# A hybrid decoder trunk on one core: small constants moved to the sync queue, the first memory and weight pieces halved, 8 leading products instead of 18

## The chip, the core and the metric

The kernel runs on one core of one Trainium2 chip. A core has five engines that run their own instruction streams in order and meet through semaphores: TensorE (matrix products; PE in the profile, its weight loads PEld), VectorE (DVE), ScalarE (ACT), GpSimd (POOL) and SyncE (SP, which here only issues transfers). Sixteen transfer engines carry data between the chip's main memory and the on-chip memory. Transfers can be issued from the sync engine, from ScalarE and from GpSimd.

The metric is the device time of one execution in microseconds (us). Before the change the median of three runs is 1012.1 us (1011.76 to 1013.38).

## What is computed

A decoder trunk of two layers on 256 tokens with 1024 channels, in float32, and a memory of 256 rows. Cut to its frame:

```python
mem_kv = rms_norm(mem, mem_norm_g) @ mem_w_kv
for i in range(2):
    x = x + 0.5 * swiglu(rms_norm(x, ffn1_norm_g[i]), ffn1_w_in[i], ffn1_w_out[i])
    hn = rms_norm(x, mix_norm_g[i])
    # layer 0: mLSTM heads; layer 1: sliding-window attention with learned sinks
    # both: 4 heads that attend to the memory, through mem_k and mem_v
    x = x + jnp.concatenate([y_tok, y_mem], axis=-1) @ w_out
    x = x + 0.5 * swiglu(rms_norm(x, ffn2_norm_g[i]), ffn2_w_in[i], ffn2_w_out[i])
```

`swiglu` multiplies by a gate half and an up half of `w_in` (2 x 2816 columns), forms silu(gate) * up, and multiplies by `w_out`. Nearly all the time is in these products and in the projections.

## The kernel before

**Products in three parts.** Every float32 weight and activation is split into a rounded high half and the remainder, the low half. A product is then three passes of TensorE: high by high, high by low, low by high (`mm3`, lines 224 to 227). A weight piece is 128 partitions by 4 chunks by 256 columns, 512 KB. `wtile` (line 216) fetches it through the sync queue into one of 5 raw buffers (`wr`), and `split` (line 206) makes the halves: ScalarE casts the high half (`wh`, line 211), VectorE subtracts to get the low half (`wl`, line 212). There are 8 buffers of each half, so the splits can run some pieces ahead of TensorE. A raw buffer is free for the next fetch when VectorE has made the low half.

**Who sets the order.** TensorE and the sync engine run in the order in which the program emits their instructions (`manual_schedule`, line 987). For ScalarE, VectorE and GpSimd a scheduler at build time fixes the order from its own model of times; on the chip these engines then run that order strictly. `issue_after` lets a block of instructions be placed no earlier than a given one. `Weave` interleaves the main chain of products with side chains (`spawn`) by an estimate of TensorE's time.

**The start.** `memory()` (line 400) computes keys and values of the memory. It first issues 18 leading products on a cleared tile (`WARM`, line 58; line 406), whose result is not used. Then it fetches the memory in four blocks of two chunks (`memT`, line 410, 256 KB each); `split_gain` (line 239) scales a chunk by the norm's gain and splits it, the high half on ScalarE (line 132), the low half on VectorE (line 241). The weights `mem_w_kv` are used in four groups of 256 columns, each 8 chunks deep. Group 0's first four chunks are fetched as two pieces of two chunks behind memory block 0, its last four as one piece behind block 2. Its first half is multiplied by `first_part` (line 323, products at line 334), which takes all high-by-high products of a piece first, so that the low halves may come later; the second half and the other groups go through `part` with `mm3`. Behind the fetches of group 1 stand those of `con` (identity, frequencies, masks), then of the other groups and the activations `xT`. The statistics of the memory's norm are a small product (line 231) and a chain on VectorE and GpSimd (lines 250, 251).

**The small constants.** `late_constants` (line 182) fetches the attention mask (196 KB), the gate bias, the sinks, the positions and two norm gains of 16 values through GpSimd's queue, copies the mask and the identity to bf16 (`maskb`, `identb`), and makes `gcut`, `nsink` and `gqk` on VectorE. It is spawned by the first feed-forward after its group 5, but the scheduler places work that waits for nothing earlier: in the profile GpSimd issues five of the fetches within the first 5 us, and the mask's at 51 us.

**The feed-forward.** `ffn_in` (line 471) runs 11 groups; a group takes four weight pieces, called quarters here (two halves of depth, each for gate and up), 24 products each, into two banks of PSUM. When a group's products are done, `hidden` (line 473), the gating, runs: two products with the norm's row on VectorE (line 476), SiLU on ScalarE, two products with the up half on VectorE (line 479), then `split_plain`: a cast on ScalarE (line 245) and a subtraction on VectorE (line 246).

```python
            for ps in waiting:
                hidden(ps)
            waiting.clear()
            if mid is not None and gi == 5:
                wv.spawn(mid())
```

Of the kernel before, what the change touches and what calls it, by code (L numbers as in the profile page):

```python
# [19 lines left out]
P = 128  # L20
# [34 lines left out]
           keys=5.5, keys_d=7.2, query=9.0, head=1.5, head_m=2.5, head_p=9.3, head_o=4.0)  # L55


WARM = 18


class Weave:
# [37 lines left out]
def tile_trunk(ctx: ExitStack, tc: tile.TileContext, a, out):  # L99
# [80 lines left out]
    gqk = mk(cst, [P, 2], F32, "gqk")  # L180

    def late_constants():
        nc.gpsimd.dma_start(mask.rearrange("p a b -> p (a b)")[:, :3 * P], a["mask"])
        nc.gpsimd.dma_start(gbias, a["a_gate_b"][0].rearrange("(s h) -> h s", h=4))
        nc.gpsimd.dma_start(sink, a["b_sinks"][0].partition_broadcast(P))
        nc.gpsimd.dma_start(posi, a["positions"][0].rearrange("(h p) -> p h", p=P))
        nc.vector.tensor_copy(identb, ident)
        nc.vector.tensor_copy(maskb, mask.rearrange("p a b -> p (a b)")[:, :3 * P])
        for i, (n, r) in enumerate((("b_q_norm_g", G_BQ), ("b_k_norm_g", G_BK))):
            nc.gpsimd.dma_start(gblk[:, i], a[n][0, :ROT].partition_broadcast(P))  # L190
            nc.vector.tensor_copy(gcut[:, i:i + 1], g(r))
        for e in range(2):
            nc.vector.memset(gcut[e * 64:e * 64 + ROT], 1.0)
        nc.vector.tensor_scalar(nsink, sink, -1.0, None, op0=ALU.mult)
        tt(out=gqk, in0=gcol[:, G_XQ:G_XQ + 2], in1=gcol[:, G_XK:G_XK + 2], op=ALU.mult)
        return
        yield

    def g(i):
        return gcol[:, i:i + 1]  # L200
# [20 lines left out]
    def wcols(w, c0, kh):  # L221
        return wtile(w.rearrange("(k p) f -> p k f", p=P)[:, kh * 4:(kh + 1) * 4, c0:c0 + 256], 4)
# [93 lines left out]
    class Group:  # L316
# [3 lines left out]
            self.ps, self.rows, self.xh, self.xl = halves(mo()), rows, xh, xl  # L320
            self.w, self.c0 = w, c0

        def first_part(self, wt):

            n = 4 // len(wt)
            for i, m, k in ((i, m, k) for q in range(len(wt)) for i in range(3) for m in range(2)
                            for k in range(q * n, q * n + n)):
                w = [t[:, k % (4 // len(wt)), m * P:(m + 1) * P] for t in wt[k * len(wt) // 4]]
                x = (self.xh, self.xl)[i == 1][k // 2][:, k % 2]
                s, mv = (w[i == 2], x) if not self.rows else (None, None)  # L330
                if self.rows:
                    ms = slice(m * P, (m + 1) * P)
                    s, mv = x[:, ms], wt[k * len(wt) // 4][i == 2][:, k % (4 // len(wt))]
                nc.tensor.matmul(self.ps[:, m], s, mv, start=i == 0 and m == 0 and k == 0, stop=False,
                                 skip_group_check=True)
                wv.now += 0.109
            yield

        def part(self, kh, wt=None):
            wt = wt or wcols(self.w, self.c0, kh)  # L340
            wt = wt if isinstance(wt, list) else [wt]
            for m in range(2):
                ms = slice(m * P, (m + 1) * P)
                for k in range(4):
                    kc = kh * 4 + k
                    h, l = self.xh[kc // 2][:, kc % 2], self.xl[kc // 2][:, kc % 2]
                    wh, wl = (w[:, k % (4 // len(wt))] for w in wt[k * len(wt) // 4])
                    if self.rows:
                        mm3(self.ps[:, m], h[:, ms], l[:, ms], wh, wl,
                            start=kc == 0 and m == 0, stop=kc == 7)  # L350
                    else:
                        mm3(self.ps[:, m], wh[:, ms], wl[:, ms], h, l,
                            start=kc == 0 and m == 0, stop=kc == 7)
                yield

# [44 lines left out]
    def memory():  # L400

        idle = tmp().rearrange("p a b -> p (a b)")[:, :T].bitcast(BF16)
        nc.vector.memset(idle, 0.0)
        bank = mo()
        for i in range(WARM):
            nc.tensor.matmul(bank, idle[:, :P], idle, start=True, stop=True, skip_group_check=True)
        wkv = a["mem_w_kv"]
        mh, ml, wfirst = [], [], []
        for c2 in range(4):
            nc.sync.dma_start(memT[c2], a["memT"][:, 2 * c2:2 * c2 + 2])  # L410
            hi, lo = unit(F32R), unit(F32R)
            for m in range(2):
                split_gain(memT[c2][:, m], g(G_MEM + 2 * c2 + m), hi[:, m], lo[:, m])
            mh.append(hi)
            ml.append(lo)
            if c2 == 0:
                v = wkv.rearrange("(k p) f -> p k f", p=P)
                wfirst.append([wtile(v[:, k:k + 2, 0:256], 2) for k in (0, 2)])
            if c2 == 2:
                wfirst.append(wcols(wkv, 0, 1))  # L420
        norm = Norm(G_MEM, rows=False)

        def keys(gi, kr):
            nc.scalar.copy(kT[gi], turn(kr))
            return
            yield

        for gi in range(2):
            gr = Group(wkv, gi * 256, mh, ml, rows=True)
            for kh in range(2):  # L430
                if gi == 0 and kh == 0:
                    yield from gr.first_part(wfirst[0])
                else:
                    yield from gr.part(kh, wfirst[kh] if gi == 0 else None)
            if gi == 0:
                first = gr
                continue
            nc.sync.dma_start(con, a["con"])
            with tc.issue_after(last[0].ins):
                for c2 in range(4):  # L440
                    norm.square(memT[c2], c2 == 0)
            norm.fold()
            wv.spawn(norm.chain(), LAT['mnorm'])
            gv = Group(wkv, 512, mh, ml, rows=True)
            yield from gv.all()
            for c2 in range(4):
                nc.sync.dma_start(xT[c2], a["xT"][:, 2 * c2:2 * c2 + 2])
            yield norm.ready
            hsc = head_scales(norm.rc, P, False)
            for i, q in enumerate((first, gr)):  # L450
                kr = tmp()
                head_norm(kr, q.ps, 2, hsc)
                wv.spawn(keys(i, kr), LAT['mkeys'] + 1.5 * i)
        for gi in range(2):
            if gi == 0:
                gr = gv
            else:
                gr = Group(wkv, 768, mh, ml, rows=True)
                yield from gr.all()
            for h in range(2):  # L460
                act(vM[:, h, gi * 256:(gi + 1) * 256], gr.ps[:, h], AF.Copy, scale=norm.rc[:, h:h + 1])
            if gi == 0:
                with tc.issue_after(last[0].ins):
                    for c2 in range(4):
                        x0.put(xT[c2])
                wv.spawn(x0.chain(LAT['x0_b']), LAT['x0'])
# [560 lines left out]
```

## Time and profile before

| | |
|---|---|
| median of 3 runs | 1012.1 us (1011.76 to 1013.38) |
| the profiled execution: its time, its span | 1012.23 us, 1010.4 us |
| VectorE's low halves, 128x1024 (line 212), each | 1196 ns mean over all forms |
| ScalarE's high halves (line 211), each | 1031 ns mean over all forms |
| weight fetches of 512 KB for the memory's keys, issue to landing | 8.0 us median |
| transfers over the span | 182.70 MB, mean 181 GB/s |

A row of the timeline reads: start and duration in us, engine, line of the kernel, operation, tile written <- tiles read, shapes, count; in brackets the engine's idle time before it and what ended that. A row of the busy times by stage reads: stretch and its length, then the busy us of each engine with the count of instructions, the granted clock, the share of the transfer engines, and GB/s. Rows of the transfer queues read: packets, MB, share of the sixteen engines' time. TensorE's products overlap in its pipeline, so a product shown as 0.28 us costs TensorE less than that: the distance between starts is its pace.

### The profile page before, as it was taken

Reading aid. Unit: us, or ns where it says so; the run is one execution under the profiler, and the core shown is the slowest. Engines: PE = TensorE matmul, PEld = TensorE weight load, DVE = VectorE, ACT = ScalarE, POOL = GpSimd, SP = SyncE. Lnnn points to the kernel's source line nnn. Section 1 sums busy time; section 2 is a strip of 40 time slices with the busy share of each in tenths; the row PEclk is TensorE's granted clock in tenths of the full one; section 3 lists DMA queues with packets and bytes.
Section 4 is the critical chain, followed back from the end, with each engine's and each line's share of the span. In section 5 each row is a group of like instructions: output and inputs, shape, how many; then the busy total and the mean of one; then the engine's idle time right before and its main releaser. Section 6 shows DMA issues by size and latency. Waiting matters only on the chain.

```text
span 1010.4 us, 20624 instructions
## 1 busy us (share of the span) xinstructions
PE 998.5 (99%) x8594; PEld 980.2 (97%) x8594; DVE 655.5 (65%) x1063; ACT 519.5 (51%) x764; POOL 35.7 (4%) x32
## 2 busy tenths in 40 slices
PE   8999999999999999999999999999999999999998
PEld 7999999999999999999999999999987899999998
DVE  6866665577856676665558666656787766666551
ACT  7754445446656554444445544544557754454440
POOL 1200000000001000000000000000121000000000
PEclk9999999999999999999999999999999999999999
DMA  9776656666644566665676666567541347666550
GB/s 308 242 245 200 192 180 185 199 183 179 184 139 133 167 210 195 200 189 170 192 206 205 189 191 201 173 197 198 182 131 66 100 131 220 198 189 185 188 170 21
DMA packets 173204, 182.70 MB, mean 181 GB/s; under 512 B 7124, under 2 KB 168328, under 8 KB 173112
## 3 DMA queue, kind: packets, MB, share of 16 engines
q1 hardware_dynamic: 171872, 179.60, 58.3%
q10 hardware_dynamic: 1016, 1.58, 0.5%
q8 instruction: 67, 1.10, 0.5%
q0 software_dynamic: 224, 0.22, 0.2%
q14 instruction: 25, 0.20, 0.1%
HBM read 180.32 MB, written 1.05 MB: 180 GB/s over the span
## 4 chain that ended last, share of the span: by engine, by line
PE 94%; DVE 3%; ACT 1%; DMA 1%; POOL 0%; issue 0%; SPq 0%; ACTq 0%
PE bank L225 30%; PE bank L226 30%; PE bank L227 30%; PE bank L231 2%; PE bank L236 1%; ACT u L132 1%; DVE wl L212 1%; DMA wr<-in_mem_w_kv_dram 1%; PE bank L961 1%; POOL col L379 0%; DVE col L930 0%; DVE u L383 0%; DVE col L591 0%; PE bank L925 0%; DVE u L946 0%
## 5 line engine op out<-in xcount | busy, mean ns | idle before, releaser
L212 DVE TENSOR_TENSOR wl<-wr,wh 128x1024 fp32r<-128x1024 f32 (+1 forms) x347 | 414.7, 1196 | 279.8 <-ACT wh L211 279.0
L211 ACT CAST wh<-wr 128x1024 fp32r<-128x1024 f32 (+1 forms) x347 | 356.8, 1031 | 393.1 <-PE bank L226 368.9
L225 PE MATMUL bank<-xh,wh 128*128 128x256 f32 x1544 | 429.1, 278 | 0.0
L226 PE MATMUL bank<-xl,wh 128*128 128x256 f32 x1544 | 426.8, 276 | 0.0
L227 PE MATMUL bank<-xh,wl 128*128 128x256 f32 x1544 | 426.8, 276 | 0.0
L226 PEld LDWEIGHTS bank<-xl,wh 128*128 128x128 f32 x1544 | 290.3, 188 | 0.1
L225 PEld LDWEIGHTS bank<-xh,wh 128*128 128x128 f32 x1544 | 290.0, 188 | 0.1
L227 PEld LDWEIGHTS bank<-xh,wl 128*128 128x128 f32 x1544 | 289.9, 188 | 0.0
L225 PE MATMUL bank<-u,wh 128*128 128x256 f32 x896 | 249.3, 278 | 0.0
L226 PE MATMUL bank<-u,wh 128*128 128x256 f32 x896 | 247.6, 276 | 0.0
L227 PE MATMUL bank<-u,wl 128*128 128x256 f32 x896 | 247.6, 276 | 0.0
L225 PEld LDWEIGHTS bank<-u,wh 128*128 128x128 f32 x896 | 168.2, 188 | 1.9 <-issue 1.7
L226 PEld LDWEIGHTS bank<-u,wh 128*128 128x128 f32 x896 | 168.4, 188 | 0.1
L227 PEld LDWEIGHTS bank<-u,wl 128*128 128x128 f32 x896 | 168.3, 188 | 0.0
L225 PE MATMUL bank<-wh,xh 128*128 128x256 f32 x208 | 59.7, 287 | 0.0
L226 PE MATMUL bank<-wl,xh 128*128 128x256 f32 x208 | 57.9, 278 | 0.0
L227 PE MATMUL bank<-wh,xl 128*128 128x256 f32 x208 | 57.9, 278 | 0.0
L476 DVE TENSOR_TENSOR t<-bank,rb 128x256 f32<-128x256 f32 x88 | 36.6, 420 | 7.3 <-PE bank L227 7.3
L225 PEld LDWEIGHTS bank<-wh,xh 128*128 128x128 f32 x208 | 39.1, 188 | 0.5 <-issue 0.3
L226 PEld LDWEIGHTS bank<-wl,xh 128*128 128x128 f32 x208 | 39.1, 188 | 0.1
L227 PEld LDWEIGHTS bank<-wh,xl 128*128 128x128 f32 x208 | 39.0, 187 | 0.0
L479 DVE TENSOR_TENSOR t<-t,bank 128x256 f32<-128x256 f32 x88 | 32.7, 412 | 1.8 <-ACT t L132 1.8
(171 smaller groups left out, 657.5 us busy)
## 6 DMA issues: line engine op xcount, KB each, us to landing
wr<-in_ffn_w_in_dram SPq DMA_DIRECT2D x176, 512.0 KB, 3.6
wr<-in_ffn_w_out_dram SPq DMA_DIRECT2D x80, 512.0 KB, 3.5
wr<-in_a_w_in_dram SPq DMA_DIRECT2D x28, 512.0 KB, 3.9
wr<-in_b_w_in_dram SPq DMA_DIRECT2D x14, 512.0 KB, 4.6
wr<-in_a_w_out_dram SPq DMA_DIRECT2D x12, 512.0 KB, 3.3
wr<-in_b_w_out_dram SPq DMA_DIRECT2D x12, 512.0 KB, 3.4
wr<-in_ffn_w_out_dram SPq DMA_DIRECT2D x16, 256.0 KB, 2.8
wr<-in_mem_w_kv_dram SPq DMA_DIRECT2D x7, 512.0 KB, 8.0
```

The source lines that it names most:

```text
L132: ins = nc.scalar.activation(*args, **kw)
L211: last[0] = nc.scalar.copy(hi[:, i * n:(i + 1) * n], src[:, i * n:(i + 1) * n])
L212: tt(out=lo[:, i * n:(i + 1) * n], in0=src[:, i * n:(i + 1) * n], in1=hi[:, i * n:(i + 1) * n].bitcast(F32), op=ALU.subtract)
L225: nc.tensor.matmul(ps, wh, xh, start=start, stop=False, skip_group_check=True)
L226: nc.tensor.matmul(ps, wh, xl, start=False, stop=False, skip_group_check=True)
L227: nc.tensor.matmul(ps, wl, xh, start=False, stop=stop, skip_group_check=True)
L231: nc.tensor.matmul(ps, lhsT, rhs, start=start, stop=stop, skip_group_check=True)
L236: nc.tensor.transpose(ps, src, ident[:k, :k])
L476: tt(out=t[:, m], in0=ps[m][:, :T], in1=x.rb, op=ALU.mult)
L479: tt(out=t[:, m], in0=t[:, m], in1=ps[m][:, T:], op=ALU.mult)
L961: nc.tensor.matmul(o[es[e], cs], vr[:, i, js], pTs[e][:, src], start=i == 0, stop=i == 1, skip_group_check=True)
```

## The change

- `late_constants` fetches its six constants through the sync queue. They stand in the sync engine's order where the routine is spawned: behind the fetch of the first quarter of group 6 of the first feed-forward. The copies and small operations on VectorE are placed after the latest weight cast at that point (`issue_after`). `gqk` is made in `memory()` instead, when `con` is fetched.
- Memory block 0 is fetched as two chunks, each followed by the weights of that chunk (128 KB each, one chunk deep). Blocks 1 to 3 stay whole, each followed by the weights of its two chunks. So group 0's weights come as five pieces of 1, 1, 2, 2 and 2 chunks, in the order of use.
- `first_part` takes a list of such pieces and is used for both halves of group 0; it now also ends the accumulation. `part` loses the case of several pieces.
- The leading products fall from 18 to 8.

```diff
-WARM = 18
+WARM = 8
...
     def late_constants():
-        nc.gpsimd.dma_start(mask.rearrange("p a b -> p (a b)")[:, :3 * P], a["mask"])
-        nc.gpsimd.dma_start(gbias, a["a_gate_b"][0].rearrange("(s h) -> h s", h=4))
-        nc.gpsimd.dma_start(sink, a["b_sinks"][0].partition_broadcast(P))
-        nc.gpsimd.dma_start(posi, a["positions"][0].rearrange("(h p) -> p h", p=P))
-        nc.vector.tensor_copy(identb, ident)
-        nc.vector.tensor_copy(maskb, mask.rearrange("p a b -> p (a b)")[:, :3 * P])
-        for i, (n, r) in enumerate((("b_q_norm_g", G_BQ), ("b_k_norm_g", G_BK))):
-            nc.gpsimd.dma_start(gblk[:, i], a[n][0, :ROT].partition_broadcast(P))
-            nc.vector.tensor_copy(gcut[:, i:i + 1], g(r))
...
+        nc.sync.dma_start(mask.rearrange("p a b -> p (a b)")[:, :3 * P], a["mask"])
+        nc.sync.dma_start(gbias, a["a_gate_b"][0].rearrange("(s h) -> h s", h=4))
+        nc.sync.dma_start(sink, a["b_sinks"][0].partition_broadcast(P))
+        nc.sync.dma_start(posi, a["positions"][0].rearrange("(h p) -> p h", p=P))
+        for i, n in enumerate(("b_q_norm_g", "b_k_norm_g")):
+            nc.sync.dma_start(gblk[:, i], a[n][0, :ROT].partition_broadcast(P))
+        with tc.issue_after(last[0].ins):
+            nc.vector.tensor_copy(identb, ident)
+            nc.vector.tensor_copy(maskb, mask.rearrange("p a b -> p (a b)")[:, :3 * P])
+            for i, r in enumerate((G_BQ, G_BK)):
+                nc.vector.tensor_copy(gcut[:, i:i + 1], g(r))
+            for e in range(2):
+                nc.vector.memset(gcut[e * 64:e * 64 + ROT], 1.0)
+            nc.vector.tensor_scalar(nsink, sink, -1.0, None, op0=ALU.mult)
...
+        def first_part(self, kh, wts):
+
+            k0 = kh * 4
+            for nk, (wh, wl) in wts:
+                for i, m, k in ((i, m, k) for i in range(3) for m in range(2) for k in range(nk)):
+                    kc = k0 + k
+                    x = (self.xh, self.xl)[i == 1][kc // 2][:, kc % 2]
+                    nc.tensor.matmul(self.ps[:, m], x[:, m * P:(m + 1) * P], (wh, wl)[i == 2][:, k],
+                                     start=i == 0 and m == 0 and kc == 0, stop=i == 2 and kc == 7,
+                                     skip_group_check=True)
+                    wv.now += 0.109
+                k0 += nk
             yield
...
+        def lead(k, nk):
+            wfirst[k // 4].append((nk, wtile(v[:, k:k + nk, 0:256], nk)))
+
         for c2 in range(4):
-            nc.sync.dma_start(memT[c2], a["memT"][:, 2 * c2:2 * c2 + 2])
             hi, lo = unit(F32R), unit(F32R)
             for m in range(2):
+                if c2 == 0:
+                    nc.sync.dma_start(memT[c2][:, m], a["memT"][:, m])
+                elif m == 0:
+                    nc.sync.dma_start(memT[c2], a["memT"][:, 2 * c2:2 * c2 + 2])
                 split_gain(memT[c2][:, m], g(G_MEM + 2 * c2 + m), hi[:, m], lo[:, m])
+                if c2 == 0:
+                    lead(m, 1)
             mh.append(hi)
             ml.append(lo)
-            if c2 == 0:
-                v = wkv.rearrange("(k p) f -> p k f", p=P)
-                wfirst.append([wtile(v[:, k:k + 2, 0:256], 2) for k in (0, 2)])
-            if c2 == 2:
-                wfirst.append(wcols(wkv, 0, 1))
+            if c2 > 0:
+                lead(2 * c2, 2)
...
             nc.sync.dma_start(con, a["con"])
+            query_key_gain()
```

## The prediction, made before the changed kernel was run

> **What bounds the kernel now.** The page comes first: the engine table, then the chain of work that ended last.
>
> ```profile
> span 1010.4 us, 20624 instructions
> PE 998.5 (99%) x8594; PEld 980.2 (97%) x8594; DVE 655.5 (65%) x1063; ACT 519.5 (51%) x764; POOL 35.7 (4%) x32
> ...
> PE 94%; DVE 3%; ACT 1%; DMA 1%; POOL 0%; issue 0%; SPq 0%; ACTq 0%
> ```
>
> TensorE sets the time. A change to loads or splits counts only where TensorE is not fed, so the busy times by stage come next.
>
> ```profile
> 1.00:5.00 4.00, 3.75 (x9) 1.34 (x10) 0.60 (x8) 1.22 (x2) 3.14 (x5) 1.00 0.62 136
> 5.00:9.00 4.00, 3.89 (x18) 2.12 (x16) 1.45 (x4) 2.74 (x6) 0.00 (x0) 1.00 1.02 233
> 9.00:15.00 6.00, 4.77 (x33) 4.00 (x32) 5.33 (x10) 4.58 (x8) 0.00 (x0) 1.00 1.08 387
> 30.00:240.00 210.00, 210.00 (x1847) 209.87 (x1847) 139.74 (x184) 107.98 (x133) 4.94 (x4) 1.00 0.68 204
> ```
>
> After the times come busy us and counts of PE, PEld, DVE, ACT and POOL, then clock, DMA share and GB/s. From 30 to 240 us, which holds the whole first feed-forward, TensorE is never idle. The idle time in reach is at the start, so the timeline of the first 20 us is third.
>
> ```profile
> 1.25 6.36 PE L406 MATMUL bank<-t 128*128 128x512 bf16 x18 [1.25 <-DVE t L403]
> ...
> 5.41 0.91 ACT L132 ACTIVATE u<-u,gcol 128x256 fp32r<-128x256 f32 x2 [3.18 <-DMA u<-in_memT_dram]
> 5.50 0.15 PEld L406 LDWEIGHTS <-t 128*128 128x128 bf16 x1 [0.28 <-issue]
> 5.92 1.19 PEld L406 LDWEIGHTS <-t 128*128 128x128 bf16 x6 [0.28 <-issue]
> 6.22 1.12 ACT L211 CAST wh<-wr 128x512 fp32r<-128x512 f32 x2
> 7.26 1.94 PE L334 MATMUL bank<-wh,u 128*128 128x256 f32 x8
> 7.55 0.17 DVE L194 TENSOR_SCALAR nsink<-sink 128x16 f32<-128x16 f32 x1 [4.46 <-DMA sink<-in_b_sinks_dram]
> ...
> 10.90 1.05 ACT L211 CAST wh<-wr 128x1024 fp32r<-128x1024 f32 x1 [0.99 <-DMA wr<-in_mem_w_kv_dram]
> 11.98 1.23 DVE L212 TENSOR_TENSOR wl<-wr,wh 128x1024 fp32r<-128x1024 f32 x1 [0.67 <-ACT wh L211]
> ...
> 12.88 1.05 ACT L211 CAST wh<-wr 128x1024 fp32r<-128x1024 f32 x1
> 13.26 0.39 PE L226 MATMUL bank<-wl,u 128*128 128x256 f32 x1 [0.87 <-DVE wl L212]
> 13.96 1.23 DVE L212 TENSOR_TENSOR wl<-wr,wh 128x1024 fp32r<-128x1024 f32 x1
> 14.24 1.05 ACT L211 CAST wh<-wr 128x1024 fp32r<-128x1024 f32 x1 [0.30 <-DMA wr<-in_mem_w_kv_dram]
> 15.32 1.22 DVE L212 TENSOR_TENSOR wl<-wr,wh 128x1024 fp32r<-128x1024 f32 x1
> 16.43 0.28 PE L225 MATMUL bank<-wh,u 128*128 128x256 f32 x1
> ...
> 17.84 0.28 PE L225 MATMUL bank<-wh,u 128*128 128x256 f32 x1
> ```
>
> Real work begins at 7.26. The vector engine stands 4.46 us behind the sink fetch. At 13.26, with 25 real products issued (24 of line 334, one of line 225), TensorE gets the low half of the second piece of group 0 and is dense from there. Between 16.43 and 17.84 lie 12 products, 0.1175 us each.
>
> **The start, worked out.** The change puts memory and weights on the sync queue in the order of use, so all 48 products of group 0 can run before TensorE needs the first half of group 1, its 49th product. What matters is when that half is ready. Ahead of its last byte stand 35 KB of gains, 1024 KB of memory, 1024 KB of weights and its own 512, 2595 KB in all. Before, the landing at 10.90 had 1827 KB up to its last byte (gains, three blocks of memory, two pieces of weights); 768 KB more at the 387 GB/s of 9 to 15 us is 2.0 us, so 12.9, which fits the cast at 12.88 that waits for nothing.
>
> From this I take off what GpSimd's five small fetches cost the transfer engines. The transfer view of the first 9 us:
>
> ```profile
> q1 hardware_dynamic: 1229, 1.46, 55.3%
> q0 software_dynamic: 131, 0.02, 17.5%
> ```
>
> 0.02 MB took 17.5% of sixteen engines for 9 us, 1.57 us of all of them, and 5 to 9 us moves 233 GB/s where 9 to 15 moves 387. I take 1.5 us off: landing at 11.4, cast 1.05 to 12.45, low half 1.22 to 13.7. Then TensorE goes dense with 49 products behind it at 13.75, against 25 at 13.26: 24 x 0.1175 less 0.49 is **2.3 us gained**. A second estimate: the next half lands 512 KB or 1.35 us later, its cast ends at 13.8, its low half starts 1.5 us sooner than 15.32. From there the vector engine works without a gap up to this row:
>
> ```profile
> 25.09 0.16 DVE L250 TENSOR_SCALAR col<-bank 128x2 f32<-128x2 f32 x1 [0.97 <-PE bank L231]
> ```
>
> There it has 0.97 us of slack, so it can follow a gain of 1.5 + 0.97, about 2.4. The two agree, and 2.3 stands.
>
> Ends: with nothing taken off, landing 12.9, ready 15.2, gain 2.8 - 1.9 = 0.9. At the other end ScalarE bounds it. If the first half block of memory, 128 KB less at the 136 GB/s of 1 to 5 us, reaches it 1.0 us before 5.41, then eight scalings (0.91 for two, near 0.41 each with their overlap, 3.3), group 0's casts (four times 0.56 from the row at 6.22) and the 1.05 end at 11.0, the low half at 12.3: gain 2.8 + 0.9, 3.7. I take the middle because the 17.5% is measured and a faster first landing is not. The sync engine's three more issues are covered by that backlog.
>
> The ten dropped leading products cost nothing themselves: eight at the 0.42 us between the rows at 5.50 and 5.92 end near 4.7, before the first weights can be cast. What they did for the clock is a rival below.
>
> **The fetches moved into the first feed-forward.** Six issues join the sync queue behind the first quarter of group 6's weights, and every later weight fetch stands behind them. The queue's own waits:
>
> ```profile
> SPq L218 <- DVE wl L212: 525.6, 225, 13.3
> ```
>
> It mostly waits for a weight slot to come free, so a few tenths to a microsecond per issue is covered; the mask cast and the sink's sign, the first to use a constant, stand behind group 5's gating, and those fetches, five raw buffers ahead of the splits, are issued well before it. If this cover were gone, the six would cost about 3 us at half a microsecond each. I put 0.
>
> **The vector queue there.** This is the dear part and the diff doesn't show it. In the program order of the kernel before, group 5's gating stands among weight splits, seven quarter pieces ahead of TensorE; before group 6's first gating come the mask cast and the next splits. In the changed order, only the first quarter of group 6 is split ahead. Then come group 4's gating, group 5's gating, the mask cast, the negated sink, and only then the second quarter. ScalarE's order is the same: both gatings, then that cast. These engines run in order, and group 5's gating needs TensorE's last product of group 5. So TensorE goes on with one quarter in stock. What lies ahead of the next, by the rows of group 5's gating now:
>
> ```profile
> 99.86 1.23 DVE L212 TENSOR_TENSOR wl<-wr,wh 128x1024 fp32r<-128x1024 f32 x1 [1.49 <-ACT wh L211]
> ...
> 101.61 0.43 DVE L476 TENSOR_TENSOR t<-bank,rb 128x256 f32<-128x256 f32 x1 [0.19 <-PE bank L227]
> 102.58 1.23 DVE L212 TENSOR_TENSOR wl<-wr,wh 128x1024 fp32r<-128x1024 f32 x1 [0.55 <-ACT wh L211]
> 103.72 0.74 DVE L479 TENSOR_TENSOR t<-t,bank 128x256 f32<-128x256 f32 x2
> 105.30 1.23 DVE L212 TENSOR_TENSOR wl<-wr,wh 128x1024 fp32r<-128x1024 f32 x1 [0.83 <-ACT wh L211]
> 106.44 0.68 DVE L246 TENSOR_TENSOR u<-t,u 128x512 fp32r<-128x512 f32 x1
> 108.02 1.23 DVE L212 TENSOR_TENSOR wl<-wr,wh 128x1024 fp32r<-128x1024 f32 x1 [0.89 <-ACT wh L211]
> 109.17 0.35 DVE L188 CAST maskb<-u 128x384 bf16<-128x384 f32 x1
> ```
>
> ```profile
> 102.45 0.63 ACT L132 ACTIVATE t<-t 128x512 f32<-128x512 f32 x1
> ...
> 105.17 0.61 ACT L245 CAST u<-t 128x512 fp32r<-128x512 f32 x1
> ```
>
> From TensorE's end of group 5: second gate product 0.43, SiLU 0.63, two up products 0.74, cast 0.61, low half 0.68, mask 0.35, sink 0.17, split 1.23: 4.84 us. The weight cast (1.05) runs beside the last vector steps. The splits now come every 2.72 us (99.86, 102.58), which is TensorE's pace per quarter; the quarter in stock and two products of the next, which need only the high half, feed it 2.95 us. **Loss 1.9 us.** Ends: 1.5 if each of five neighbours overlaps by 0.08, as 109.17 begins before 108.02 plus 1.23; 2.6 if the seven changes of engine or instruction cost 0.1 each. After it the splits take 1.23 against 2.72, so the stock fills again.
>
> **Sum**, against the profiled execution's 1012.23 (span 1010.4 and 1.8 around it; the median of the runs is 1012.1): 1012.23 - 2.3 + 1.9 = **1011.8**.
>
> **The rivals.** First, *the front gains all that ScalarE allows*: 3.7 gained, 1.5 lost, 1010.0. For it: the vector engine loses its 4.46 us wait and both engines start sooner. Against it: 1 to 5 us moves only 136 GB/s, and the transfer view of 3.7 to 5 us has hardly a GpSimd packet that could be to blame:
>
> ```profile
> q0 software_dynamic: 21, 0.00, 0.9%
> ```
>
> Second, *the front is bound by bytes anyway*: gain 0.9, loss 1.9, 1013.2. For it: the engines are full (1.02) in 5 to 9 us. Against it: part of that fullness is the 17.5%. The Trainium skill, "DMA: Bandwidth & Descriptors", section "Issuing engines are not separate DMA queues", says that all issuers share the same sixteen engines, so a new issuer saves only sequencer time; by that rule the 1.5 us would come from the later moment of the fetches alone, and no run here yet shows that.
>
> Third, on the other side, *TensorE's clock opens late*. Its rate, not the clock column (1.00 throughout), shows this: the leading products come every 0.42 us until 5.92, 4.67 us after the first, then six in 1.19. Eight end near 4.7, before that point. If TensorE then falls idle and has to earn its rate anew from its dense start at 13.7, 4.67 us run at half rate: 2.3 us lost, 1014.1. With 0.4 to give away, the change is slower than before from 0.8 us of dense work at half rate. Against it: at half rate two chunks' 12 products take 2.8 us, while their 512 KB arrive in 1.35 us, so TensorE would be busy, not idle, from its first product on and open the clock before 13.7. The Trainium skill, "TensorE: Matmul & The Clock Gate", section "Part 1: The HAM clock gate", gives about 3.4 us of sustained activity in a window that runs freely; by that rule eight products are just one window long and may miss it. The trace agrees that the rate doubles after some microseconds (4.67); no run here shows the window.
>
> That the fetches don't move is excluded: the built kernel's GpSimd queue holds none.
>
> **How the numbers follow.** Forecast 0.54 (own range 1010.5 to 1013.2, from the ends of gain and loss without their corners), first rival 0.22, second 0.12, third 0.12. The range 1009.4 to 1014.3 takes in both far cases and a few tenths of spread. 0.2%, 2 us, is about what a measurement of this kernel can tell from no change: two thirds of the first rival (0.15) and a fifth of the forecast (0.11) fall below 1010.1, 0.26 faster; two thirds of the third (0.08) and tails of the second and the forecast (0.08) above 1014.1, 0.16 slower; 0.58 within.
>
> **What will show it.** Right: no sink wait on the vector engine before its first split; all 48 products of group 0 issued chunk by chunk from the leading routine; the dense start near 13.7; one TensorE wait of 1.5 to 2.6 us on the weights' low half, near 102 us, and no transfer ending a wait there. Wrong: products still 0.23 us apart after 10 us; no such wait near 102; or the chain's piece at 25.09 not 2 us sooner.

## The result: 5.7 us slower

The changed kernel takes 1017.75 us in the median of 4 runs (1016.72 to 1018.66), the kernel before 1012.03 beside it (1011.76 to 1013.38): a ratio of 1.0049, interval 1.0026 to 1.0071 (this is not the quotient of the two medians). The forecast was 1011.8, its range 1009.4 to 1014.3. The prediction was wrong: the change goes the other way, and the time lies outside the range.

The profiled execution of the changed kernel took 1018.22 us, 6.0 more than that of before. Its page, in the lines that answer to those shown of before:

```profile
span 1016.4 us, 20613 instructions
PE 1001.7 (99%) x8584; PEld 984.9 (97%) x8584; DVE 655.9 (65%) x1065; ACT 519.9 (51%) x766; POOL 30.9 (3%) x26
...
PE 91%; DVE 4%; ACT 2%; DMA 1%; POOL 1%; issue 1%; SPq 0%; ACTq 0%; DVEq 0%; POOLq 0%
```

The span grew by 6.0, yet TensorE's busy time grew by 3.2, although it issues ten products fewer. That is the first hint that waits are only a part. The busy times by stage, columns as before:

```profile
1.00:5.00 4.00, 3.75 (x10) 1.42 (x11) 1.38 (x10) 2.09 (x4) 0.00 (x0) 1.00 0.64 169
5.00:9.00 4.00, 2.02 (x13) 1.59 (x13) 1.99 (x6) 2.42 (x6) 0.00 (x0) 0.93 0.88 270
9.00:15.00 6.00, 5.77 (x37) 5.56 (x37) 4.65 (x9) 4.66 (x8) 0.00 (x0) 0.76 1.05 369
30.00:240.00 210.00, 208.34 (x1787) 207.80 (x1786) 134.79 (x179) 102.93 (x127) 3.30 (x3) 1.00 0.65 198
```

From 30 to 240 us TensorE is idle for 1.66 us, but issues 60 products fewer than before (1787 against 1847) in the same 210 us. 1.66 us is room for about 15 products; the other 45 are missing while TensorE counts as busy at a granted clock of 1.00.

**The start.** The timeline of the first 25 us:

```profile
6.44 0.48 PE L334 MATMUL bank<-wl,u 128*128 128x256 f32 x2
...
7.32 0.91 ACT L132 ACTIVATE u<-u,gcol 128x256 fp32r<-128x256 f32 x2 [1.51 <-DMA u<-in_memT_dram]
...
8.79 2.08 PE L334 MATMUL bank<-wh,u 128*128 128x256 f32 x8 [1.87 <-ACT wh L215]
...
12.75 1.05 ACT L215 CAST wh<-wr 128x1024 fp32r<-128x1024 f32 x1 [0.76 <-DMA wr<-in_mem_w_kv_dram]
...
13.83 1.23 DVE L216 TENSOR_TENSOR wl<-wr,wh 128x1024 fp32r<-128x1024 f32 x1 [1.11 <-ACT wh L215]
...
15.11 0.39 PE L230 MATMUL bank<-wl,u 128*128 128x256 f32 x1 [0.34 <-DVE wl L216]
...
24.12 0.16 DVE L254 TENSOR_SCALAR col<-bank 128x2 f32<-128x2 f32 x1
```

The sink wait on VectorE is gone and products start at 4.62 instead of 7.26, but then TensorE stands for 1.87 us until memory block 1 has come. The first half of group 1 is cast at 12.75, where 11.4 had been forecast for its landing (12.88 before); TensorE is dense from 15.11 instead of 13.75. The statistics row of the memory's norm, at 25.09 before, stands at 24.12: 0.97 gained, not 2.3. In between the clock stood at half, from 8.4 to 11.8 us:

```profile
8.00:9.00 1.00, 0.21 (x1) 0.21 (x2) 0.98 (x3) 0.94 (x3) 0.00 (x0) 0.71 1.04 349
9.00:10.00 1.00, 1.00 (x5) 1.00 (x6) 1.00 (x3) 1.00 (x3) 0.00 (x0) 0.50 0.93 299
...
11.00:12.00 1.00, 1.00 (x7) 1.00 (x6) 0.79 (x2) 0.89 (x2) 0.00 (x0) 0.59 1.09 385
```

**The wait near 104.** The timeline there, first VectorE's rows, then the two of TensorE that begin after a wait:

```profile
99.25 0.43 DVE L481 TENSOR_TENSOR t<-bank,rb 128x256 f32<-128x256 f32 x1 [6.21 <-PE bank L231]
100.61 0.43 DVE L481 TENSOR_TENSOR t<-bank,rb 128x256 f32<-128x256 f32 x1 [0.93 <-PE bank L231]
101.73 0.75 DVE L484 TENSOR_TENSOR t<-t,bank 128x256 f32<-128x256 f32 x2 [0.70 <-ACT t L132]
103.23 0.69 DVE L250 TENSOR_TENSOR u<-t,u 128x512 fp32r<-128x512 f32 x1 [0.74 <-ACT u L249]
103.84 0.35 DVE L191 CAST maskb<-u 128x384 bf16<-128x384 f32 x1
104.11 0.17 DVE L196 TENSOR_SCALAR nsink<-sink 128x16 f32<-128x16 f32 x1
104.18 5.76 DVE L216 TENSOR_TENSOR wl<-wr,wh 128x1024 fp32r<-128x1024 f32 x5
...
104.20 0.39 PE L229 MATMUL bank<-xh,wh 128*128 128x256 f32 x1 [0.91 <-ACT wh L215]
...
105.46 0.39 PE L231 MATMUL bank<-xh,wl 128*128 128x256 f32 x1 [0.76 <-DVE wl L216]
```

This is the stall that the prediction had worked out, near its place, in its order and size: gating, mask, sink, then the split. TensorE stands first for the high half (0.91), whose cast comes behind ScalarE's part of the gating, and two products later for the low half (0.76), 1.67 us in all; the prediction had counted the high half as there in time. Five splits follow back to back, and no later wait stands up to 240 us.

**The rest.** Counts of products in two stretches of the first feed-forward in which TensorE never waits, first of the kernel before:

```profile
60.00:100.00 40.00, 40.00 (x355) 40.00 (x355) 25.77 (x35) 19.97 (x23) 0.00 (x0) 1.00 0.61 190
115.00:220.00 105.00, 105.00 (x929) 105.00 (x928) 64.72 (x80) 51.30 (x62) 0.00 (x0) 1.00 0.64 186
```

then of the changed kernel:

```profile
60.00:100.00 40.00, 40.00 (x355) 40.00 (x355) 19.20 (x29) 13.15 (x16) 0.00 (x0) 1.00 0.47 138
115.00:220.00 105.00, 105.00 (x894) 105.00 (x893) 64.71 (x79) 51.48 (x62) 0.00 (x0) 1.00 0.66 201
```

Up to 100 us both issue 355; after the wait the changed kernel issues 894 where 929 went before. The starts of products lie 0.1133 us apart in the one and 0.1178 in the other, evenly, at the same clock, and stay so to the end of the feed-forward. The two paces are called fast and slow below.

A clock a few per cent lower, which the column doesn't show, would look alike, and no run here excludes it. There is a hint against it: TensorE's weight loads in the feed-forward take 188 ns in the fast pace and 330 at half clock (from 9.3 to 11.5 us), but in the slow pace two of three still take 188, and that of the second pass 192. As ends of TensorE's records are modelled in the profile, it is no more than a hint.

What the feed-forward lost can be read between two fixed places, the first products after the norm's broadcast and after the next norm's statistics. The timeline of before, then of the changed kernel:

```profile
55.27 0.28 PE L226 MATMUL bank<-xl,wh 128*128 128x256 f32 x1
...
224.37 0.28 PE L226 MATMUL bank<-xl,wh 128*128 128x256 f32 x1
```

```profile
54.28 0.28 PE L230 MATMUL bank<-xl,wh 128*128 128x256 f32 x1
...
230.27 0.28 PE L230 MATMUL bank<-xl,wh 128*128 128x256 f32 x1
```

169.10 us became 175.99, 6.9 more. 1053 products from 105.68 on at 0.0045 more each are 4.7; the other 2.2 are put down to the wait and the slower first products behind it. With 1.0 gained at the start this is 5.9 of the 6.0; after 236 us the two traces run alike.

### The profile page after: what moved, and what is told of

It reads as the page before. It is cut to its first block, busy times and chain, and to the rows that moved or that the text cites. A ratio compares the mean times of both kernels' runs of the same rounds, so it can differ in the third digit from the quotient of the medians.

```text
span 1016.4 us, 20613 instructions
## 1 busy us (share of the span) xinstructions
PE 1001.7 (99%) x8584; PEld 984.9 (97%) x8584; DVE 655.9 (65%) x1065; ACT 519.9 (51%) x766; POOL 30.9 (3%) x26
## 4 chain that ended last, share of the span: by engine, by line
PE 91%; DVE 4%; ACT 2%; DMA 1%; POOL 1%; issue 1%; SPq 0%; ACTq 0%; DVEq 0%; POOLq 0%
PE bank L229 30%; PE bank L231 29%; PE bank L230 29%; PE bank L235 2%; ACT u L132 1%; DVE wl L216 1%; POOL col L379 1%; PE bank L240 1%; DMA wr<-in_mem_w_kv_dram 1%; DVE u L951 0%; DVE col L935 0%; PE bank L966 0%; DMA u<-in_memT_dram 0%; DVE u L383 0%; ACT wh L215 0%
## 5 line engine op out<-in xcount | busy, mean ns | idle before, releaser
L216 DVE TENSOR_TENSOR wl<-wr,wh 128x1024 fp32r<-128x1024 f32 (+2 forms) x349 | 414.5, 1190 | 270.2 <-ACT wh L215 269.5
L215 ACT CAST wh<-wr 128x1024 fp32r<-128x1024 f32 (+2 forms) x349 | 356.6, 1025 | 382.0 <-PE bank L230 354.4
L132 ACT ACTIVATE t<-t 128x512 f32<-128x512 f32 x44 | 27.6, 627 | 21.7 <-DVE t L481 21.7
```

The lines of the kernel that those rows point to most:

```text
L132: ins = nc.scalar.activation(*args, **kw)
L215: last[0] = nc.scalar.copy(hi[:, i * n:(i + 1) * n], src[:, i * n:(i + 1) * n])
L216: tt(out=lo[:, i * n:(i + 1) * n], in0=src[:, i * n:(i + 1) * n], in1=hi[:, i * n:(i + 1) * n].bitcast(F32), op=ALU.subtract)
```

## The experiments

Three theories stood at first for the 4.7 us. P: TensorE has two paces and takes up one of them at each interruption of its stream of products. W: only the waits count, and the pace is an artefact. C: the slow pace comes from the refill behind the wait, when transfers and splits catch up. Times are medians, the ratios are to the kernel before on the same chip (medians 1012.2 to 1012.32), with their intervals, again not the quotients of the medians.

**Fetches early.** The changed kernel, but the six fetches go on the sync queue at the end of `memory()`; the vector operations stay in `late_constants`, without `issue_after`.

```diff
-    def late_constants():
+    def fetch_constants():
         nc.sync.dma_start(mask.rearrange("p a b -> p (a b)")[:, :3 * P], a["mask"])
...
-        with tc.issue_after(last[0].ins):
...
+    def late_constants():
+        nc.vector.tensor_copy(identb, ident)
...
                 wv.spawn(x0.chain(LAT['x0_b']), LAT['x0'])
+        fetch_constants()
```

> The changed kernel with the six fetches on the sync queue at the end of the memory's stage instead of behind group 5; the vector queue then keeps its lead over TensorE in group 5. Theory P (a wait makes TensorE resume at 0.1178 us a product instead of 0.1133, until other products come between): no wait near 105 us, 0.1133 from 54 to 230 us, the start's gain of 1.0 us stays: about 1011. Rival C (TensorE is slower after 105 us because the transfers that refill the buffers share memory with it): also near 1011, since nothing has to be refilled. Rival W (the wait near 105 us costs its 1.7 us and the rest was lost elsewhere): 1016.

Measured: 1019.73, ratio 1.0048 (1.0027 to 1.0069). The wait near 105 is gone. In its place the mask cast and the sink's sign now stand among the statistics' steps on VectorE at 30 us, and TensorE waits 2.0 us for a low half, up to 34.7, behind which the clock is at half from 35.1 to 38.5. In the profiled execution the pace is slow from 57.4 to 239 us. The ten times fall in two heaps, 1013.4 to 1015.2 (four) and 1019.7 to 1021.6 (six). The distance, about 6.4 between their medians, is near what 1488 products at 0.0045 make, 6.7 (these are fast in the kernel before and slow here). That the two heaps are the two paces is inferred from this; only one execution has a trace.

**A broadcast ahead of group 7.** The changed kernel with four short products (the norm's row broadcast once more, result unused) some 70 products behind the wait.

```diff
+            if mid is late_constants and gi == 7:
+                bcast_rows(mo(), x.rc)
```

> The changed kernel with the norm's broadcast products (line 235's two calls, into a bank that nobody reads) issued once more ahead of group 7. The wait near 105 us and the refilling stay. Theory P: TensorE goes back to 0.1133 there, some 960 products at 0.0045 less are 4.3 us, less 0.4 for the added products: 1013.8. Rivals C and W: the pace stays 0.1178 until 230 us, 1018.1.

Measured: 1018.48, ratio 1.0058 (1.0043 to 1.0073): missed. The wait is as in the changed kernel, but behind it the pace was fast (0.1135 over 69 products), and slow (0.1178 over 983) from the inserted broadcast on. Up to group 7 this is the changed kernel, whose trace is slow behind the same wait: the pace changes at an interruption, but the wait does not say which pace follows, and the same instructions can run in either.

**Statistics products ahead of group 2, in the kernel before.** Four one-column products, nothing waits for them.

```diff
+            if mid is late_constants and gi == 2:
+                pc = mo()
+                for h in range(2):
+                    mmf(pc[:, h:h + 1], x.acc[:, 0, h * P:(h + 1) * P], ones, 1)
```

> The kernel before with the norm's column products (ones, one column each, into a bank that nobody reads) issued once more ahead of group 2. In every feed-forward's end of both traces, these products are followed by 0.1178. Nothing waits, no transfer moves. Theory P: 0.1178 from group 2 to the end of the first feed-forward, some 1390 products at 0.0045 more are 6.3 us, plus 0.4: 1018.7. Rivals C and W: 1012.4.

Measured: 1019.18, ratio 1.0069 (1.0054 to 1.0084), as P had it. Busy times by stage:

```profile
60.00:100.00 40.00, 40.00 (x343) 40.00 (x342) 26.22 (x37) 19.75 (x25) 0.00 (x0) 1.00 0.59 186
115.00:220.00 105.00, 105.00 (x894) 105.00 (x894) 62.67 (x78) 48.88 (x59) 0.00 (x0) 1.00 0.59 181
```

The same 894 products, with no wait in the feed-forward, no fetch moved and 181 GB/s against 186. W and C fall: the pace alone costs 7 us here. (The profiled execution, 1021.09, is the longest of the four; in it the clock also fell at the start, from 14.5 to 17.9 us, and the statistics row came at 27.06.)

**The changed start alone.** Halves and 8 leading products, with the constants on GpSimd's queue at once, as before.

```diff
-        nc.sync.dma_start(sink, a["b_sinks"][0].partition_broadcast(P))
+            nc.gpsimd.dma_start(sink, a["b_sinks"][0].partition_broadcast(P))
...
```

> The start of the changed kernel (halves, order of use, 8 leading products), with the six fetches on GpSimd as before; the vector queue stands behind the sink fetch again, and has the order of before in the first feed-forward. Theories P, C and W alike: no wait near 105 us and 0.1133 there. The start alone: between 1.0 us gained, as in the changed kernel, and 1 us lost, if the sink wait holds the first low halves: 1011 to 1013.

Measured: 1013.15, ratio 1.0002 (0.9993 to 1.0012). Fast pace from 55 to 224 us, no wait there. VectorE stands behind the sink again, the statistics row is at 25.18 (25.09 before). Halves and fewer leading products gain nothing by themselves; the whole loss hangs on the fetches. The clock column misses something here: it shows 1.00, but from 7.4 to 13.9 us the products come 0.213 us apart, twice the normal distance.

**One broadcast in the kernel before, ahead of group 2.**

```diff
+            if mid is late_constants and gi == 2:
+                bcast_rows(mo(), x.rc)
```

> The kernel before with one extra broadcast of the norm's row (four short products, result unused) ahead of group 2 of the first feed-forward. Nothing waits for it. If a broadcast swaps TensorE's pace (fast 0.1133 us a product, slow 0.1178), the some 1460 products after it are slow: 1012.2 + 0.4 + 6.6 = 1019.2. If a broadcast always leaves the fast pace behind, 1012.6. If the paces are not set by interruptions at all, 1012.6 too.

Measured: 1019.15, ratio 1.0059 (1.004 to 1.0078). Five executions took 1018.9 to 1020.8, the profiled one 1013.15. In that one the products after the statistics at 46 us were fast for once (slow in the kernel before), the norm's own broadcast at 55 made them slow, the inserted one at 58 fast again. So each broadcast swapped the pace, and the pace in which TensorE came to the first of them decided the rest.

**The fetches alone.** The kernel before with its own start, and the constants on the sync queue behind the first quarter of group 6.

```diff
-        nc.gpsimd.dma_start(sink, a["b_sinks"][0].partition_broadcast(P))
+        nc.sync.dma_start(sink, a["b_sinks"][0].partition_broadcast(P))
...
```

> The kernel before with the moved fetches alone: its own start (block 0 and the pieces whole, 18 leading products), the six constants on the sync queue behind the first quarter of group 6. Bytes theory: the whole gain of the start is that the vector engine no longer stands behind the sink, and the first half of group 1 lands when it did; the statistics row (25.09 before, 24.12 after) comes at 24.1 to 24.4, and the wait of 1.5 to 2.2 us stands near 104; then 1013.3 in the fast pace or 1017.8 in the slow one. Halves theory: the row stays near 25.0 and the time is 0.8 longer in either case.

Measured: 1017.3 (1014.88 to 1019.72), ratio 1.0045 (1.0028 to 1.0062). The timeline has the statistics row sooner than in the changed kernel:

```profile
23.76 0.16 DVE L254 TENSOR_SCALAR col<-bank 128x2 f32<-128x2 f32 x1 [0.82 <-PE bank L235]
```

1.33 gained against 0.97: neither theory's number. The transfers moved 270 GB/s from 2 to 9 us (207 before, 247 in the changed kernel), so taking GpSimd's fetches out of the start does speed it up, and the halves seem to give a part back (more on that below; the row of the changed start varies by half a microsecond by itself, 23.58 in the run with early fetches against 24.12). The wait near 104 is there (0.90 + 0.76 us), and behind it stood something new, the clock at half for 3.4 us, from 105.2 to 108.6:

```profile
105.00:106.00 1.00, 0.91 (x4) 0.91 (x5) 1.00 (x2) 1.00 (x2) 0.00 (x0) 0.59 0.00 0
106.00:107.00 1.00, 1.00 (x7) 1.00 (x6) 1.00 (x2) 1.00 (x2) 0.00 (x0) 0.50 0.56 172
...
108.00:109.00 1.00, 1.00 (x8) 1.00 (x8) 1.00 (x2) 0.45 (x1) 0.00 (x0) 0.70 0.70 162
```

Fifteen products came 0.213 us apart instead of 0.113, 1.5 us lost; then the pace was slow. So a wait of 1.7 us can cost itself, half a clock and a pace, and the four times spread over 4.8 us.

**18 leading products in the changed kernel.** `WARM = 18`.

> The changed kernel with 18 leading products in place of 8. Bytes theory: TensorE's products between 8.8 and 12.6 us come twice as fast, but its dense start stays where the first half of group 1 lands (15.1), and the statistics row at 24.1: 1017.7. Clock theory: the half rate held the start back, and the row comes up to 1.5 us sooner: 1016.2. Either with the slow pace after the wait near 105; with the fast pace 4.7 less.

Measured: 1016.67 (1014.99 to 1018.45), ratio 1.0039 (1.0026 to 1.0053). Inconclusive for the start: the clock stayed at 1.00 up to 19 us, but the row came at 25.54, later than either theory had it. The transfers moved only 251 and 246 GB/s from 8 to 10 us in this execution (349 and 299 in the changed kernel's), and TensorE waited 1.4 us for a high half at 13.7. Behind the wait near 106 it had half a clock and then the fast pace: the changed kernel's order does not force the slow one.

**The sink's sign on GpSimd.** The kernel before with one instruction moved, so that VectorE has no 4.46 us wait.

```diff
-        nc.vector.tensor_scalar(nsink, sink, -1.0, None, op0=ALU.mult)
+        nc.gpsimd.tensor_scalar(nsink, sink, -1.0, None, op0=ALU.mult)
```

> The kernel before with one instruction moved: the sink's sign is changed on GpSimd, not on the vector engine, so the vector engine has no 4.46 us wait for the sink; no fetch moves. If that wait is what the start gains: the statistics row at 24.1, fast pace as before, no wait near 105: 1011.2. If GpSimd's transfers cost the start: the row at 24.6 to 25.1, 1011.7 to 1012.2. If the shifted start leaves the slow pace from 55 us on: 1017.8.

Measured: 1013.72 (1011.61 to 1021.05, 12 runs), ratio 1.0017 (1.0004 to 1.0031): slower, and at none of the three numbers. The row is at 26.27, 1.2 later than before. Busy times by stage:

```profile
10.00:12.00 2.00, 0.70 (x6) 0.49 (x4) 0.68 (x3) 1.27 (x2) 0.00 (x0) 1.00 1.07 388
12.00:13.00 1.00, 0.21 (x1) 0.01 (x1) 1.00 (x2) 0.87 (x3) 0.00 (x0) 0.85 1.08 385
13.00:14.00 1.00, 0.91 (x4) 0.92 (x5) 1.00 (x4) 0.76 (x1) 0.00 (x0) 0.50 1.08 391
...
15.00:16.00 1.00, 1.00 (x6) 1.00 (x6) 1.00 (x3) 1.00 (x3) 0.00 (x0) 0.50 1.09 386
```

The products that the wait had held back now run early, the bytes come no sooner, so TensorE is busy for only 0.91 of the 3 us from 10 to 13. The clock then falls to half from 12.7 to 16.1 us.

**The same with that gap filled.** Nine more products on the cleared tile behind the first half of group 0.

```diff
                     yield from gr.first_part(wfirst[0])
+                    for i in range(9):
+                        nc.tensor.matmul(bank, idle[:, :P], idle, start=True, stop=True, skip_group_check=True)
```

> The run with the sink's sign on GpSimd again, with nine more products on the cleared tile (0.21 us each, result unused) behind the first half of group 0, where TensorE stood idle (0.90 of 3 us busy from 10 to 13). Clock theory: idle time there let the clock fall to half from 12.8 to 16.1; filled, the clock stays 1.00, the products keep 0.118 us apart and the statistics row is back at 24.9 to 25.2: 1012.1. If idle time isn't the cause, the half rate stays and the row is at 26.3 or later: 1013.7.

Measured: 1012.22 (1011.97 to 1012.88), ratio 0.9996 (0.9987 to 1.0005), the row at 25.20:

```profile
10.00:12.00 2.00, 2.00 (x12) 1.14 (x13) 0.51 (x2) 0.98 (x2) 0.00 (x0) 1.00 1.08 390
...
13.00:14.00 1.00, 0.63 (x5) 0.63 (x6) 1.00 (x3) 1.00 (x1) 0.00 (x0) 1.00 1.08 389
...
15.00:16.00 1.00, 1.00 (x11) 1.00 (x10) 0.99 (x3) 1.00 (x3) 0.00 (x0) 1.00 1.08 382
```

Filled, the clock stays at 1.00 and the loss is gone: the idle time was the cause. The executions without a trace bear it out by their mean clock. With the sink's sign on GpSimd it was 0.996 to 0.998 in 11 of 12, filled 0.999 or 1.000 in all ten. The kernel before itself shows 0.997 or 0.998 in 23 of the 79 executions beside these runs, and these took 1013.6 to 1014.2, the others but one 1011.7 to 1012.6; so the clock seems to fall in its start too, now and then. The one left took 1019.29 at a mean clock of 1.000, 7 us more, as if in the slow pace.

**Late fetches on GpSimd.** The kernel before; a small copy from the norm's row into each of the five tiles makes their fetches wait until about 50 us on GpSimd's own queue, and the sink's sign is on GpSimd.

```diff
+        for t in (gbias, sink, posi, gblk[:, 0], gblk[:, 1]):
+            nc.gpsimd.tensor_copy(t[:, :2], x0.rc[:t.shape[0]])
         nc.gpsimd.dma_start(gbias, a["a_gate_b"][0].rearrange("(s h) -> h s", h=4))
...
-        nc.vector.tensor_scalar(nsink, sink, -1.0, None, op0=ALU.mult)
+        nc.gpsimd.tensor_scalar(nsink, sink, -1.0, None, op0=ALU.mult)
```

> The kernel before with the five small fetches held back on GpSimd's own queue until the norm's row of the first feed-forward is there (about 48 us), and the sink's sign changed on GpSimd. The sync queue, the vector engine's and ScalarE's orders stay as before. If the gain of the start comes from taking GpSimd's transfers out of it, and the loss of the changed kernel from the vector order alone: the statistics row at 23.8 (23.76 in the run with the fetches alone), no wait of TensorE from 30 to 240 us, fast pace, 1010.9. If TensorE's idle time at the start lets the clock fall to half as in the run with the sink's sign on GpSimd: row 25.3 to 26.3, 1012.4 to 1013.5. If late fetches disturb the feed-forward: a wait between 50 and 110 us.

Measured: 1011.19 (1010.28 to 1012.92, 11 runs), ratio 0.9988 (0.9979 to 0.9997): a little faster than the kernel before. In the timeline and the stages of the profiled execution, the shortest of the eleven:

```profile
23.28 0.16 DVE L252 TENSOR_SCALAR col<-bank 128x2 f32<-128x2 f32 x1 [0.55 <-PE bank L233]
```

```profile
115.00:220.00 105.00, 105.00 (x929) 105.00 (x928) 65.42 (x82) 51.11 (x63) 0.00 (x0) 1.00 0.64 188
```

The start gains 1.8 there, 0.4 of it because the first 94 dense products ran in the fast pace (slow in the kernel before); 281 GB/s from 2 to 9 us, no wait from 26 to 240 us, 929 products again.

**The same late fetches, with the changed start** (halves, 8 leading products).

> The same late fetches on GpSimd, with the changed kernel's start: block 0 and the pieces in halves, 8 leading products. If halves and fewer leading products bring something once the sink wait is gone: row before 23.8, below 1010.9. If they cost, since the raw buffers are all taken and the clock is at half from 8.7 to 11.6 us: row at 24.1 as in the changed kernel, 1011.2, no wait from 30 to 240 us.

Measured: 1011.59 (1011.31 to 1012.11, 11 runs), ratio 0.9994 (0.9986 to 1.0003). The row is at 24.54, the clock at half from 8.4 to 11.9 us, no wait from 26 to 240 us, fast pace. Beside the run before it, halves and 8 products cost 1.3 us at the row of the profiled executions, pace included, and 0.4 in the medians. Beside the changed kernel, which has the same start, 6.2 us are gone: with the fetches off the sync queue VectorE's order is that of before, and the wait and the slow pace don't come.

**The broadcast twice**, ahead of groups 2 and 3 of the kernel before.

```diff
+            if mid is late_constants and gi in (2, 3):
+                bcast_rows(mo(), x.rc)
```

> The kernel before with the extra broadcast of the norm's row twice, ahead of group 2 and ahead of group 3 of the first feed-forward. In the twelve profiled runs so far and the kernel before, a broadcast between long stretches of products swapped the pace every time (63 times from slow to fast, 4 times from fast to slow). If it swaps, the second one puts back what the first one changed: slow for the 96 products of group 2 alone (0.4), two broadcasts (0.4 each), 1013.4, with most executions near it, where one broadcast gave 1019.15. If an extra broadcast leaves the slow pace whatever came before, 1019.5.

Measured: 1013.47 (1013.02 to 1015.17, 10 runs), ratio 1.0009 (0.9993 to 1.0025). Busy times by stage in group 2, and later:

```profile
62.00:70.00 8.00, 8.00 (x71) 8.00 (x69) 4.86 (x6) 3.19 (x5) 0.00 (x0) 1.00 0.60 190
115.00:220.00 105.00, 105.00 (x929) 105.00 (x928) 64.89 (x80) 50.60 (x60) 0.00 (x0) 1.00 0.61 187
```

The starts lie 0.1178 apart between the two broadcasts and 0.1133 after the second, which took back what one alone had cost (1019.15). That a broadcast swaps the pace is shown.

## Why the prediction was wrong, step by step

- *What bounds the kernel*: right. TensorE stayed the bound; no transfer ended a wait of it in the feed-forward.
- *The fetches on the sync queue at nothing*: right. No transfer was missed around 100 us: the sync queue stood for up to 21.2 us waiting for a split to free a raw buffer.
- *The vector queue, 1.9 lost (1.5 to 2.6)*: right in order and size, nearly in place. 1.67 us show as idle, 2.2 with the restart. It had one wait for the low half near 102; there are two near 104, the first and longer one for the high half.
- *The start, 2.3 gained*: mis-sized, 0.97. The 1.5 us for GpSimd's transfers held. The run with the gap filled and the one with late fetches both keep VectorE free of the sink and the clock at 1.00, and GpSimd issues the five fetches in both, early in the one, late in the other: the row is at 25.20 and 23.28, 1.9 sooner, 0.4 of it by the pace. So the later moment suffices, and the other issuer is not needed. The Trainium skill, "DMA: Bandwidth & Descriptors", section "Issuing engines are not separate DMA queues", says that the transfers of all issuers run on the same sixteen engines, so that another issuer saves only time on the sequencer. The traces agree with that, by these 1.9 us. What failed is "the sync engine's three more issues are covered by that backlog", by which the halves cost nothing. With whole pieces and no early fetch of GpSimd, the first half of group 1 was cast at 11.48 and 11.69 (late fetches, fetches alone), where 11.4 had been forecast for its landing; with halves at 12.22 to 14.35 in five traces, 12.75 in the changed kernel's, 0.13 sooner than before. The halves gave back what the later fetches had gained. By what is not shown: the half was issued at 6.07 instead of 4.97, but by 6.0 the transfers had moved only 0.85 of the 2.1 MB ahead of it, at 172 and 211 GB/s from 5 to 7 us.
- *Second rival, the front bound by bytes*: its gain of 0.9 is what the start measured, by luck: it let GpSimd's fetches cost nothing, while they did cost 1.5 and the halves took that away again. Its whole time, 1013.2, still lacks 4.7.
- *Third rival, the clock opens late*: half happened. The argument against it, "TensorE would be busy, not idle, from its first product on", was wrong: block 1 came late, TensorE stood from 6.9 to 8.8, and the clock was at half until 11.8. Two of the prediction's own signs of being wrong came true: products 0.213 us apart after 10 us, and the piece at 25.09 less than 2 us sooner. The price was small, since the first half of group 1 came only at 12.75. The Trainium skill, "TensorE: Matmul & The Clock Gate", section "Part 1: The HAM clock gate", puts the fall behind an idle window of about 3.4 us; here 1.9 us of it sufficed, and with the sink's sign on GpSimd 2.1 us broken by one product, while 1.94 in the run with early fetches did not. The measurement decides. That the window runs freely, as the page says, fits that the same wait near 104 kept the clock in one run and halved it in another.
- *The sum*: here the prediction failed. It took the wait as the only cost of the stall and every product outside it at the pace of before; its 2.72 us per quarter was used as a constant of TensorE. It is a pace held since the last interruption, and both paces stood in the prediction's own figures: 0.1175 us a product at the start, and 2.72 for 24 products, 0.1133, in the feed-forward. The stall was a new interruption, slow products followed, and 1053 of them at 0.0045 made 4.7 us, the largest term and in no rival. With the measured terms the sum is 1012.2 - 1.0 + 2.2 + 4.7 = 1018.1 against 1018.22. Without the 4.7, if the fast pace had followed the wait as in two other traces, an estimate is 1013.5: slower than before even so, but inside the range.

The runs show that an interruption can change the pace and what that costs. Why TensorE settles on one or the other isn't known. In the thirteen traces before the last run, from the distances over a dozen products on either side: 67 broadcasts between stretches of products swapped the pace every time; 92 groups of statistics products left the slow pace 89 times (74 after fast, 15 after slow). Behind the wait both were seen. No experiment tried what in TensorE holds the pace.

## What to carry to other kernels

When a change moves instructions on a helper engine so that the bound engine stops once in a long dense stretch, price the restart too: the wait, perhaps half a clock for 3.4 us, and the pace of every product up to the next interruption. Before removing a wait ahead of a start that is bound by bytes, ask whether the work it held back kept TensorE awake; if so, fill the gap. To keep small transfers out of a crowded start, hold them back on the queue they already use, which leaves the order of the other engines alone.

## What the runs showed of the hardware

- Products of 128x128 by 256 columns have two steady paces at a granted clock of 1.00, 0.1133 and 0.1178 us, kept for up to 1488 products in a row. Four short products in between are enough to change it, and the same instructions can run in either: behind the same wait near 104 the changed kernel was slow, and the run that differs from it only from group 7 on was fast.
- The granted clock fell to 0.50 for 3.4 us after 1.6 to 2.2 us of idle TensorE (up to two products in between) in eight traces, in the middle of a kernel that had been dense for 50 us as well (15 products 0.213 us apart). It did not fall every time: 1.67 us near 104 and 1.94 at the start also passed without it.
- Five fetches of 25 KB in all, issued by GpSimd in the first 5 us, cost the start about 1.3 to 1.5 us.
